# Two-layer hybrid encoder in float32 on one core: conditioning columns load into idle tiles during the feed-forward, and its Strassen sums are gated in the last chunk

## The chip, the cores and the metric

The kernel runs on one core of one Trainium2 chip. The metric is the device time of one execution in microseconds (us); lower is better. The kernel before takes 1888.2 us, the median of three runs between 1886.48 and 1891.04 us.

## What is computed

The reference is a trunk of two layers on one sequence of 512 tokens with 1024 channels, in float32. Cut to what matters here, a layer is:

```python
mod = (silu(c) @ ada_w[l] + ada_b[l])            # six vectors of 1024 from the conditioning vector c
shift_m, scale_m, gate_m, shift_f, scale_f, gate_f = split(mod, 6)
h = rms_norm(x, norm_mix_g[l]) * (1 + scale_m) + shift_m
y = ...                                          # two attention branches, gates, output projection
x = x + gate_m * y
h = rms_norm(x, norm_mlp_g[l]) * (1 + scale_f) + shift_f
x = x + gate_f * (square(relu(h @ w_mlp_up[l])) @ w_mlp_down[l])
```

The last line is the feed-forward: 1024 channels up to 4096 and down to 1024 again. Its result is multiplied by the vector `gate_f` and added to the residual `x`. The six vectors `mod` of a layer are made in 48 pieces of 128 values; the kernel calls each piece a column.

## The kernel before

**Numbers.** Every float32 matrix is split into a high part and a low remainder of a type that TensorE multiplies at full rate, and a product is three matmuls: high by high, high by low, low by high (`mm3`, L265). Each weight tile therefore takes a DMA into a row tile `raw`, an ACT copy to `wh` and a DVE subtraction to `wl` (`split_w`, L249).

**Columns.** `ada` (L141) makes one column. It loads 128 rows of `ada_w` by 1024 (512 KB) into a tile `raw` and DVE multiplies and sums it with the conditioning row in one instruction (the profile's CUSTOM_DVE_ANT_0). Unless told otherwise the tile comes from the pool `rawp`, four buffers that the weight loads use as well.

**Feed-forward.** The loop of L1106 goes over eight chunks `fc` of 512 hidden channels. A chunk first makes its hidden rows (`ups`: four weight tiles `w_up`, 24 matmuls each, then relu, square and split on ACT and DVE), then multiplies them by its part of `w_down`. In chunks below `SEVEN` (six chunks of layer 0, seven of layer 1) this second product is done by Strassen's scheme as seven block products instead of eight. For it DVE forms sums of four `w_down` tiles (`columnside`, two of them in `rawp`), and of the hidden rows (`rowside`). `down7` (L1049) runs the seven products, and `take` moves their results from PSUM into eight sums `y` of 128x512 in SBUF, DVE adding each to what is there. One of the seven products (a12 by b21) is needed only in the first block of the result; it is never moved, and stays in two PSUM banks `zb` of the pool `accp` through all Strassen chunks. `down7` takes the columns of this chunk as a list and calls one at four places (`spare`).

The other chunks are plain. Two row tiles of `w_down` per half of the channels (`cc`) are split, then for each of four blocks `t` of 128 tokens twelve matmuls fill a PSUM bank from `acc()` (two banks of `accp`, three of `ssp`); DVE multiplies the bank by the gate row `gf`, and POOL, in the last chunk DVE, adds it to the residual `x1`. Layer 0 has two plain chunks (6 and 7), layer 1 one (7).

**Where the two meet (L1118).** At the first plain chunk the kernel adds `zb` to the first two sums, multiplies all eight sums by `gf` on DVE and adds them to `x1` on POOL. After the tiles of a plain chunk come its columns (L1172): ten of them in chunk 6 of layer 0.

**Order.** Instructions are handed to a planner, which orders each engine's queue by its own estimate of time, earlier program text first where several could start, and gives out buffers as they become free. Each engine and the DMA queue of SP then run strictly in that order. Only between `order(True)` and `order(False)` is the order that of the text: from the second half of the output projection to the first three `up` blocks, and from the second half (`cc` = 1) of the last chunk of layer 0 through the attention of layer 1, where the RMSNorm of the next layer is woven between the tiles (`norms`, L1160). A column's DVE instruction may not run ahead of the last such stretch (`floor`, L155).

**The pair.** The pool `pp` (L54) has two buffers of 128x1024. Attention uses it for its probabilities; in the feed-forward it holds only the gate row, `gm` during the output projection and `gf` (`grow`, L325) from the first plain chunk on.

Of the kernel before, what the change touches and what calls it, by code (L numbers as in the profile page):

```python
# [10 lines left out]
F32 = mybir.dt.float32  # L11
# [8 lines left out]
D = 1024  # L20
# [4 lines left out]
FCH = 4  # L25
# [16 lines left out]
def trunk(ctx, tc, x, c, pos, cols, rows, ada_w, w_qkv, w_gate, w_ba, w_bb, w_out, w_up, w_down, out):  # L42
# [8 lines left out]
    rawp = pool("raw", 4)  # L51
    wp = pool("w", 5)
    halfp = pool("half", 10)
    pp = pool("p", 2)  # L54
    sp = pool("scr", 2)
    accp = pool("acc", 2, PS)
    ssp = pool("ss", 3, PS)
    tpp = pool("tp", 2, PS)
# [3 lines left out]
    def nosync(after, before):  # L62
        tc.add_manual_dep(after.ins, before.ins.name,
                          mybir.DependencyInfo(mybir.DependencyClass.NoSync,
                                               mybir.DependencyReason.DATA), reason="order")
# [23 lines left out]
    T_, V_, S_, G_ = Ordered(nc.tensor), Ordered(nc.vector), Ordered(nc.scalar), Ordered(nc.gpsimd)  # L89
# [3 lines left out]
    big = lambda shape, dt, name: bigp.tile(shape, dt, name=name, tag="big")  # L93
    turns = [0]

    def acc(wide=True):
        turns[0] += 1
        if wide and turns[0] % 5 >= 2:
            return ssp.tile([128, 512], F32, name="acc", tag="s")
        return accp.tile([128, 512], F32, name="acc", tag="acc")  # L100
# [37 lines left out]
        E_.dma_start(xt, src[t])  # L138
        return xt

    def ada(l, j, far=False, pool_=False):  # L141
        raw = big([128, D], F32, "raw") if far else rawp.tile([128, D], F32, name="raw", tag="raw")
        E_.dma_start(raw, ada_w[l, j])
        m, bias = modT[l][:, j:j + 1], adab[l][:, j:j + 1]

        def add():
            S_.activation(raw, raw, AF.Copy, accum_out=m)
            V_.tensor_add(m, m, bias)

        if pool_:  # L150
            G_.tensor_mul(raw, raw, cbc)
            return add
        else:
            ins = V_.tensor_tensor_reduce(raw, raw, cbc, 1.0, bias, OP.mult, OP.add, m)
            if floor[0] is not None:  # L155
                nosync(ins, floor[0])
# [108 lines left out]
    def mm3(o, sh, sl, mh, ml, start, stop, **more):  # L265
        matmul(o, sh, mh, start=start, stop=False, **more)
        matmul(o, sh, ml, start=False, stop=False, **more)
        matmul(o, sl, mh, start=False, stop=stop, **more)
# [333 lines left out]
    SEVEN = (6, 7)  # L602
# [7 lines left out]
    def prepare(l):  # L610
        hT = []
        return hT, [qkv(l, p, int(p < 6), hT) for p in range(NB_Q)]
# [32 lines left out]
    def first_products(nT, turn, hT, pieces, gslots):  # L645
# [4 lines left out]
        def scales(kt):  # L650
            ada(0, 8 + kt, True)
# [65 lines left out]
    for l in range(DEPTH):  # L717
# [161 lines left out]
        x1 = {}  # L879
        zT = []  # L880
        wb = None
        for j in range(KT):
# [10 lines left out]
            wh, wl = split_w(w_ba[l, j], scale=sg[:, l:l + 1])  # L893
# [5 lines left out]
            zb = sp.tile([128, 512], F32, name="zb", tag="f512", bufs=6)  # L899
# [14 lines left out]
        for cc in range(2):  # L914
# [6 lines left out]
            for t in range(NT):  # L921
                if cc == 0:
                    x1[t] = load_x(t, xsrc)
                ps = acc()
                tk = slice(128 * t, 128 * t + 128)
                for kt in range(KT):
                    wh, wl = w[kt // 2]
                    cw = slice(512 * (kt % 2), 512 * (kt % 2) + 512)
                    mm3(ps, zT[kt][:, 0, tk], zT[kt][:, 1, tk], wh[:, cw], wl[:, cw], kt == 0, kt == KT - 1)
                d = sp.tile([128, 512], F32, name="d", tag="f512", bufs=6)  # L930
# [38 lines left out]
        upturn = [0]  # L969

        def ubank():
            upturn[0] += 1
            pool_, tag = ((ssp, "s"), (pvp, "pv"))[upturn[0] % 2]
            return pool_.tile([128, 512], F32, name="acc", tag=tag)

        def product(banks, u, w, start):

            wh, wl = w
            for i, ps in enumerate(banks):
                for k in range(2):  # L980
                    tk = slice(256 * k + 128 * i, 256 * k + 128 * i + 128)
                    cw = slice(512 * k, 512 * k + 512)
                    mm3(ps, u[:, 0, tk], u[:, 1, tk], wh[:, cw], wl[:, cw], start and k == 0, k == 1,
                        skip_group_check=not start)

        ys, qs, uT, zb = {}, {}, [], []
# [51 lines left out]
        def columnside(fc):  # L1038

            r11, r12, t1, t2 = (big([128, 1024], F32, "raw") for _ in range(4))  # L1040
            r21, r22 = (rawp.tile([128, 1024], F32, name="raw", tag="raw") for _ in range(2))
            for r, (j, k) in ((r11, (0, 0)), (r12, (0, 1)), (r22, (1, 1)), (r21, (1, 0))):
                E_.dma_start(r, w_down[l, fc, k, j])
            V_.tensor_sub(t1, r12, r11)
            V_.tensor_sub(t2, r22, t1)
            V_.tensor_sub(r12, r22, r12)
            return r11, r21, t2, t1, r12, r22
# [48 lines left out]
            take((1, 0), xb)  # L1096


        todo = [lambda i=i: ada(l, i) for i in range(40, 48)]
        counts = [2, 1, 1, 1, 1, 1, 1]  # L1100
        if l + 1 < DEPTH:
            todo += [lambda i=i: ada(l + 1, i) for i in range(24)]
            counts = [3, 3, 4, 4, 4, 4, 10]
        fill = {l: {fc: [todo.pop(0) for _ in range(n)] for fc, n in enumerate(counts)}}

        for fc in range(FC):  # L1106
            last = fc == FC - 1
            if seven(fc):
                w7 = columnside(fc)
            ups(fc, (2, 3) if fc and seven(fc - 1) else range(FCH))  # L1110
            if fc == SEVEN[l]:
                gf = grow(l, 1)
            if seven(fc):
                u7 = rowside(fc)
                ups(fc + 1, (0, 1))
                down7(fc, u7, w7, fill[l].pop(fc, []))
                continue
            if fc == SEVEN[l]:  # L1118
                for b, y in zip(zb, ys[0, 0]):
                    V_.tensor_add(y, y, b)  # L1120
                for (i, cc), y2 in sorted(ys.items()):
                    for k, y in enumerate(y2):
                        xs = slice(512 * cc, 512 * cc + 512)
                        V_.tensor_mul(y, y, gf[:, xs])
                        G_.tensor_add(x1[2 * i + k][:, xs], x1[2 * i + k][:, xs], y)
            if last and l + 1 < DEPTH:
                nxt = prepare(l + 1)
                for i in range(2):
                    nxt[1][0]["load"](i, True)
            for cc in range(2):  # L1130
                w = [split_w(w_down[l, fc, cc, i]) for i in range(2)]
                if last and l + 1 < DEPTH and cc == 0:
                    nxt[1][0]["load"](2)
                ahead = last and cc == 1 and l + 1 < DEPTH
                if ahead:
                    pairs = halves(nxt[0])
                    aT = affine(l + 1, 0)
                    norms = []
                    order(True)
                    nxt[1][0]["load"](3)  # L1140
                for t in range(NT):
                    tk = slice(128 * t, 128 * t + 128)
                    d = sp.tile([128, 512], F32, name="d", tag="f512", bufs=6)
                    final = last and l == DEPTH - 1 and cc == 1 and t == NT - 1
                    for lo, hi in ((0, 256), (256, 512)) if final else ((0, 512),):
                        ps = acc()[:, lo:hi]
                        for f in range(FCH):
                            wh, wl = w[f // 2]
                            cw = slice(512 * (f % 2) + lo, 512 * (f % 2) + hi)
                            mm3(ps, uT[f][:, 0, tk], uT[f][:, 1, tk], wh[:, cw], wl[:, cw], f == 0, f == FCH - 1)  # L1150
                        xs = slice(512 * cc + lo, 512 * cc + hi)
                        V_.tensor_mul(d[:, lo:hi], ps, gf[:, xs])
                        (V_ if last else G_).tensor_add(x1[t][:, xs], x1[t][:, xs], d[:, lo:hi])
                        if last and l == DEPTH - 1:
                            E_.dma_start(out[t, :, xs], x1[t][:, xs])
                    if last and l + 1 < DEPTH and cc == 0:
                        ms[t] = msp.tile([128, 2], F32, name="ms2", tag="ms")
                        square(x1[t], ms[t], 0)
                    if ahead:
                        norms.append(norm(l + 1, 0, t, x1[t], ms[t], aT, pairs))  # L1160
                        if t > 1:
                            norms[t - 2][2]([0])
                        norms[t][0]()
                        E_.dma_start(x2d[t], x1[t])
                        if t > 0:
                            norms[t - 1][1]()
                        if t > 1:
                            norms[t - 2][2]([1])
                if ahead:
                    norms[3][1]()  # L1170
                    early = {1 + i: norms[2 + i][2] for i in range(2)}
            for f in fill[l].pop(fc, []):  # L1172
                f()


_ORDER = ["x", "c", "pos", "cols", "rows", "ada_w", "w_qkv", "w_gate", "w_ba", "w_bb", "w_out", "w_up",
# [64 lines left out]
```

## Time and profile before

| What | Value |
|---|---|
| median of three runs | 1888.2 us |
| the profiled execution, its own time | 1888.52 us |
| its span, first to last instruction | 1886.7 us |
| mean granted TensorE clock | 0.992 |
| ACT, busy | 1021.4 us, 54% of the span |
| DMA, read from memory | 205.09 MB |
| feed-forward of layer 0 | about 613 to 964 us |
| feed-forward of layer 1 | about 1553 to 1883 us |

A row of the groups view names an engine, an operation, the tile written and the tiles read, the shape and the count; behind it stand the busy time, the mean time of one in ns, the idle time of the engine just before such instructions, and what ended it. PE is TensorE, PEld its weight load, DVE VectorE, ACT ScalarE, POOL GpSimd, SP the engine whose queue issues the loads; SPq is that queue. L81 stands on every row, because a helper that records each operation sits there; tile names tell the rows apart. In the view of windows each row is a stretch of time: its length, then for PE, PEld, DVE, ACT and POOL the busy time and the number of instructions, then the granted clock, the busy share of the DMA engines and GB/s. `y` in the attention is another tile than the sums `y` of the feed-forward; the shape 128x512 marks the latter.

### The profile page before, as it was taken

What the parts mean: (1) busy time and instruction counts of PE and PEld (TensorE: products, weight loads), DVE (VectorE), ACT (ScalarE), POOL (GpSimd) and SP (SyncE); (2) the same over time, 40 slices, a digit from 0 to 9 for tenths busy, and PEclk for the clock granted to TensorE, in tenths of its full rate; (3) what the DMA queues carried; (4) which work ended last, traced back from release to release, by engine and by line L of the source; (5) the groups of instructions that cost most, each with busy time, mean ns of one, the idle gap of its engine ahead of it and who ended that gap; (6) DMA issues with size and microseconds to landing.
All of it is one profiled execution on the core that took longest, in us unless ns stands there. A gap on an engine that the chain in (4) does not pass through costs nothing.

```text
span 1886.7 us, 27295 instructions
## 1 busy us (share of the span) xinstructions
PE 1846.5 (98%) x9988; PEld 1632.2 (87%) x9988; DVE 1323.5 (70%) x2357; ACT 1021.4 (54%) x2309; POOL 375.0 (20%) x447
## 2 busy tenths in 40 slices
PE   7999999999999999999899999999999999999998
PEld 5999999998888887878689999999888888888887
DVE  8664567777565778889675465787646567788887
ACT  5565667776434544444355655777662345545541
POOL 4332224422020000001424232343210200000002
PEclk8999999999999999999899999999999999999999
DMA  8421211224563444445322121122136534333331
GB/s 301 136 68 51 60 44 59 61 66 149 201 216 126 135 141 151 151 148 172 118 99 89 35 76 52 42 68 71 45 112 203 190 110 134 123 101 121 102 101 67
DMA packets 63639, 212.09 MB, mean 112 GB/s; under 512 B 7185, under 2 KB 7569, under 8 KB 63506
## 3 DMA queue, kind: packets, MB, share of 16 engines
q1 hardware_dynamic: 63218, 210.27, 34.2%
q8 instruction: 79, 1.29, 0.3%
q14 instruction: 54, 0.44, 0.1%
q10 hardware_dynamic: 288, 0.09, 0.0%
HBM read 205.09 MB, written 5.24 MB: 111 GB/s over the span
## 4 chain that ended last, share of the span: by engine, by line
PE 46%; DVE 10%; DMA 4%; ACT 3%; issue 2%; POOL 1%; DVEq 0%; ACTq 0%; POOLq 0%
PE acc L81 39%; DVE wl L81 3%; PE tp L81 2%; DVE y L81 2%; DVE raw L81 2%; PE s L81 2%; DMA raw<-in_ada_w 2%; PE pv L81 2%; DMA raw<-in_w_up 1%; PE pvb L81 1%; DMA raw<-in_w_down 1%; ACT wh L81 1%; DVE uT L81 1%; DVE s L81 1%; POOL rs L81 1%
## 5 line engine op out<-in xcount | busy, mean ns | idle before, releaser
L81 PE MATMUL acc<-wh,hT 128*128 128x384 f32 x1792 | 517.8, 346 | 6.0 <-ACT hT L81 5.1
L81 ACT ACTIVATE wh<-raw 128x1024 fp32r<-128x1024 f32 (+1 forms) x331 | 324.0, 987 | 321.5 <-PE acc L81 179.1
L81 DVE TENSOR_TENSOR wl<-raw,wh 128x1024 fp32r<-128x1024 f32 (+1 forms) x331 | 378.2, 1153 | 157.9 <-ACT wh L81 157.0
L81 PE MATMUL acc<-hT,wh 128*128 128x512 f32 (+1 forms) x1632 | 482.8, 379 | 5.3 <-ACT wh L81 5.2
L81 PEld LDWEIGHTS acc<-hT,wh 128*128 128x128 f32 x1632 | 298.9, 189 | 61.3 <-ACT wh L81 6.8
L81 PEld LDWEIGHTS acc<-wh,hT 128*128 128x128 f32 x1792 | 330.6, 189 | 12.0 <-ACT hT L81 6.2
L81 PE MATMUL acc<-wh,uT 128*128 128x512 f32 (+1 forms) x928 | 296.4, 393 | 11.1 <-DVE uT L81 7.3
L81 PE MATMUL acc<-hT,wl 128*128 128x512 f32 (+1 forms) x816 | 306.1, 378 | 0.8 <-DVE wl L81 0.7
L81 PE MATMUL acc<-wl,hT 128*128 128x384 f32 x896 | 303.1, 338 | 0.8 <-DVE wl L81 0.8
L81 PEld LDWEIGHTS acc<-wh,uT 128*128 128x128 f32 x928 | 176.0, 190 | 49.8 <-DVE uT L81 8.1
L81 POOL TENSOR_TENSOR rs<-ms,half_neg 128x4 f32<-128x4 f32 (+1 forms) x128 | 123.2, 963 | 476.0 <-DVE ms L81 474.8
L81 PE MATMUL acc<-wl,uT 128*128 128x512 f32 (+1 forms) x464 | 181.1, 390 | 0.0
L81 PEld LDWEIGHTS acc<-hT,wl 128*128 128x128 f32 x816 | 153.6, 188 | 29.9 <-DVE wl L81 1.8
L81 PEld LDWEIGHTS acc<-wl,hT 128*128 128x128 f32 x896 | 169.8, 190 | 4.8 <-DVE wl L81 1.9
L81 DVE CUSTOM_DVE_ANT_0 raw<-raw,cbc,colt 128x1024 f32<-128x1024 f32 x94 | 124.5, 1333 | 52.5 <-DMA raw<-in_ada_w 52.3
L81 POOL TENSOR_TENSOR xt<-xt,y 128x512 f32<-128x512 f32 x16 | 27.4, 1742 | 586.5 <-DVE y L81 586.5
L81 ACT ACTIVATE p<-s,nm 128x512 f32<-128x512 f32 x128 | 86.8, 684 | 64.4 <-DVE nm L81 64.4
L81 PEld LDWEIGHTS acc<-wl,uT 128*128 128x128 f32 x464 | 88.2, 190 | 18.0
L81 DVE TENSOR_TENSOR y<-y,acc 128x512 f32<-128x512 f32 x144 | 94.8, 680 | 11.1 <-PE acc L81 10.6
L81 DVE TENSOR_REDUCE nm<-s 128x1 f32<-128x512 f32 x128 | 82.2, 684 | 28.0 <-PE s L81 27.3
L81 ACT ACTIVATE wT<-tp 128x512 f32<-128x512 f32 (+1 forms) x128 | 65.9, 541 | 45.7 <-PE tp L81 45.7
L81 ACT ACTIVATE T<-y 128x128 fp32r<-128x128 f32 x224 | 68.6, 357 | 39.3 <-POOL y L81 39.3
(158 smaller groups left out, 2820.8 us busy)
## 6 DMA issues: line engine op xcount, KB each, us to landing
raw<-in_ada_w SPq DMA_DIRECT2D x96, 512.0 KB, 4.2
raw<-in_w_qkv SPq DMA_DIRECT2D x112, 384.0 KB, 3.2
raw<-in_w_up SPq DMA_DIRECT2D x64, 512.0 KB, 3.6
raw<-in_w_down SPq DMA_DIRECT2D x64, 512.0 KB, 3.5
raw<-in_w_gate SPq DMA_DIRECT2D x32, 512.0 KB, 3.6
raw<-in_w_ba SPq DMA_DIRECT2D x16, 512.0 KB, 4.4
raw<-in_w_out SPq DMA_DIRECT2D x16, 512.0 KB, 4.1
xt<-in_x SPq DMA_DIRECT2D x8, 512.0 KB, 5.7
```

The source lines that it names most:

```text
L81: ins = f(*a, **k)
```

## The change

Four things are changed. First, the 32 columns made in the feed-forward of layer 0 (eight of its own gate, 24 of layer 1) and the eight of layer 1 load into `pp` in place of `rawp`, four in each of the six Strassen chunks of layer 0 and eight in chunk 6, one after each tile, where it was three, three, four, four, four, four and ten after the tiles. Second, the plain chunk 6 of layer 0 is not gated: its tiles are added to the sums `y` by DVE, and its first two tiles go on accumulating in the held banks `zb`. Third, in the last chunk of each layer every tile is preceded by its own sum's part: DVE multiplies `y` by `gf` and adds it to `x1`; the first two tiles accumulate in `zb` and are gated with it. POOL does none of these adds any more. Fourth, since `zb` keeps the two banks of `accp`, the tiles take banks from `dbank` (`ssp` and `tpp`) until the second half of the last chunk.

```diff
-    def ada(l, j, far=False, pool_=False):
-        raw = big([128, D], F32, "raw") if far else rawp.tile([128, D], F32, name="raw", tag="raw")
+    def ada(l, j, far=False, pool_=False, aside=False):
+        if aside:
+            raw = pp.tile([128, D], F32, name="raw", tag="p")
+        else:
+            raw = big([128, D], F32, "raw") if far else rawp.tile([128, D], F32, name="raw", tag="raw")
...
+        def dbank():
+            upturn[0] += 1
+            pool_, tag = ((ssp, "s"), (tpp, "tp"), (tpp, "tp"))[upturn[0] % 3]
+            return pool_.tile([128, 512], F32, name="acc", tag=tag)
...
-        todo = [lambda i=i: ada(l, i) for i in range(40, 48)]
+        todo = [lambda i=i: ada(l, i, aside=True) for i in range(40, 48)]
         counts = [2, 1, 1, 1, 1, 1, 1]
         if l + 1 < DEPTH:
-            todo += [lambda i=i: ada(l + 1, i) for i in range(24)]
-            counts = [3, 3, 4, 4, 4, 4, 10]
+            todo += [lambda i=i: ada(l + 1, i, aside=True) for i in range(24)]
+            counts = [4, 4, 4, 4, 4, 4, 8]
...
-            if fc == SEVEN[l]:
-                for b, y in zip(zb, ys[0, 0]):
-                    V_.tensor_add(y, y, b)
-                for (i, cc), y2 in sorted(ys.items()):
-                    for k, y in enumerate(y2):
-                        xs = slice(512 * cc, 512 * cc + 512)
-                        V_.tensor_mul(y, y, gf[:, xs])
-                        G_.tensor_add(x1[2 * i + k][:, xs], x1[2 * i + k][:, xs], y)
+            extra = fill[l].pop(fc, [])
...
                 for t in range(NT):
                     tk = slice(128 * t, 128 * t + 128)
-                    d = sp.tile([128, 512], F32, name="d", tag="f512", bufs=6)
                     final = last and l == DEPTH - 1 and cc == 1 and t == NT - 1
+                    y = ys[t // 2, cc][t % 2]
+                    if last:
+                        xs = slice(512 * cc, 512 * cc + 512)
+                        d = sp.tile([128, 512], F32, name="d", tag="f512", bufs=6)
+                        V_.tensor_mul(y, y, gf[:, xs])
+                        V_.tensor_add(x1[t][:, xs], x1[t][:, xs], y)
+                    held = cc == 0 and t < 2
                     for lo, hi in ((0, 256), (256, 512)) if final else ((0, 512),):
-                        ps = acc()[:, lo:hi]
+                        ps = zb[t] if held else (acc() if last and cc else dbank())[:, lo:hi]
...
+                        if not last:
+                            if not held:
+                                V_.tensor_add(y, y, ps)
+                            if extra:
+                                extra.pop(0)()
+                            continue
                         xs = slice(512 * cc + lo, 512 * cc + hi)
                         V_.tensor_mul(d[:, lo:hi], ps, gf[:, xs])
-                        (V_ if last else G_).tensor_add(x1[t][:, xs], x1[t][:, xs], d[:, lo:hi])
+                        V_.tensor_add(x1[t][:, xs], x1[t][:, xs], d[:, lo:hi])
...
-            for f in fill[l].pop(fc, []):
-                f()
```

More of the change, by code (lines that the diff above doesn't have):

```diff
@@ L1149, in trunk @@
                             cw = slice(512 * (f % 2) + lo, 512 * (f % 2) + hi)
-                            mm3(ps, uT[f][:, 0, tk], uT[f][:, 1, tk], wh[:, cw], wl[:, cw], f == 0, f == FCH - 1)
+                            mm3(ps, uT[f][:, 0, tk], uT[f][:, 1, tk], wh[:, cw], wl[:, cw], f == 0 and not held,
+                                f == FCH - 1, skip_group_check=held)
+                        if not last:
[4 more added lines that the diff above has]
+                            continue
                         xs = slice(512 * cc + lo, 512 * cc + hi)
                         V_.tensor_mul(d[:, lo:hi], ps, gf[:, xs])
-                        (V_ if last else G_).tensor_add(x1[t][:, xs], x1[t][:, xs], d[:, lo:hi])
+                        V_.tensor_add(x1[t][:, xs], x1[t][:, xs], d[:, lo:hi])
                         if last and l == DEPTH - 1:
```

## The prediction

> **What bounds the kernel now.** I read the page's engine table first, then PE's waits, then the windows chunk by chunk, then the load queue.
>
> ```profile
> PE 1846.5 (98%) x9988; PEld 1632.2 (87%) x9988; DVE 1323.5 (70%) x2357; ACT 1021.4 (54%) x2309; POOL 375.0 (20%) x447
> ```
>
> TensorE sets the time. The change adds and removes no matmul, so it can gain only where PE stands still or runs slowly in the two feed-forwards. The windows, by chunk: six stretches of the Strassen chunks of layer 0, its passage to the plain chunks, an undisturbed stretch of layer 1, and the end.
>
> ```profile
> 613.00:655.00 42.00, 41.22 (x233) 35.87 (x231) 32.79 (x44) 24.35 (x41) 0.00 (x0) 1.00 0.43 133
> 655.00:696.00 41.00, 40.48 (x177) 33.16 (x178) 32.91 (x41) 20.96 (x30) 0.00 (x0) 1.00 0.41 132
> 696.00:739.00 43.00, 41.07 (x181) 33.72 (x181) 36.28 (x47) 19.89 (x26) 0.00 (x0) 1.00 0.47 147
> 739.00:786.00 47.00, 47.00 (x201) 38.44 (x201) 39.99 (x51) 20.86 (x28) 0.00 (x0) 0.96 0.49 148
> 786.00:824.00 38.00, 36.60 (x161) 29.68 (x160) 32.42 (x41) 18.60 (x25) 0.00 (x0) 1.00 0.45 145
> 824.00:869.00 45.00, 45.00 (x200) 37.26 (x199) 39.53 (x54) 23.18 (x31) 0.00 (x0) 1.00 0.42 138
> 869.00:920.00 51.00, 42.31 (x174) 33.95 (x173) 44.10 (x51) 12.89 (x17) 24.68 (x15) 0.87 0.57 188
> 1655.00:1696.00 41.00, 41.00 (x182) 33.98 (x181) 33.04 (x42) 19.99 (x27) 0.00 (x0) 1.00 0.36 116
> 1858.00:1887.00 29.00, 22.03 (x108) 18.18 (x106) 23.54 (x27) 1.55 (x4) 13.45 (x8) 0.99 0.20 73
> ```
>
> In 1655 to 1696 PE does 182 matmuls in 41.00 us, 0.2253 us each; that is the pace without a stop. By it the matmuls of the other stretches would take 177 × 0.2253 = 39.9 of 41 us, 40.8 of 43, 45.3 of 47, 36.3 of 38, 45.1 of 45: a loss of 1.1, 2.2, 1.7, 1.7 and 0, together 6.7 us. In 613 to 655, where small transposes lie between, I take the idle time, 0.8 us. In 869 to 920 the 174 would take 39.2 of 51: 11.8 us lost, to waits and to a clock granted at 0.87. PE's waits say for what, in layer 0 and then in layer 1:
>
> ```profile
> PE acc L81 <- ACT wh L81: 5.2, 2, 4.4
> PE acc L81 <- DVE uT L81: 4.3, 1, 4.3
> PE acc L81 <- DVE y L81: 3.8, 3, 1.9
> ...
> PE acc L81 <- DVE uT L81: 3.0, 1, 3.0
> ```
>
> So 0.8 + 6.7 + 11.8 + 3.0 = 22.3 us is all that there is to win.
>
> **Why the Strassen chunks of layer 0 lose 7.5 us, and layer 1 none.** The load queue, one chunk of layer 0, its passage, one chunk of layer 1, and DVE's groups in the Strassen chunks of either layer:
>
> ```profile
> 736.43 8.50 SPq L81 DMA_DIRECT2D raw<-in_w_up  x4
> 748.28 7.84 SPq L81 DMA_DIRECT2D raw<-in_ada_w  x4
> 759.27 8.56 SPq L81 DMA_DIRECT2D raw<-in_w_down  x4
> ...
> 871.22 16.38 SPq L81 DMA_DIRECT2D raw<-in_ada_w  x10
> 894.10 12.29 SPq L81 DMA_DIRECT2D raw<-in_w_up  x4
> ...
> 1643.03 0.33 SPq L81 DMA_DIRECT2D raw<-in_ada_w  x1
> 1645.66 15.80 SPq L81 DMA_DIRECT2D raw<-in_w_down  x4
> ```
> ```profile
> L81 DVE TENSOR_TENSOR raw<-raw 128x1024 f32<-128x1024 f32 x24 | 29.2, 1219 | 7.1 <-DMA raw<-in_w_down 7.0
> L81 DVE CUSTOM_DVE_ANT_0 raw<-raw,cbc,colt 128x1024 f32<-128x1024 f32 x22 | 28.2, 1282 | 14.3 <-DMA raw<-in_ada_w 14.3
> ...
> L81 DVE CUSTOM_DVE_ANT_0 raw<-raw,cbc,colt 128x1024 f32<-128x1024 f32 x6 | 7.7, 1285 | 4.5 <-DMA raw<-in_ada_w 4.4
> ```
>
> The four row tiles are given out in the order of the text. In layer 0 four columns stand between the `w_up` tiles and the next `w_down` tiles; DVE, which works in order, waits 14.3 us for them and 7.0 us for the `w_down` behind them, and what it has queued behind those waits is the adds to `y` that free PE's banks. In layer 1 one column stands there, and PE stops nowhere. With the columns in the pair, a chunk asks for six row tiles, not ten. I take the 7.5 us as gone. What would be late next is DVE itself: with four columns of 1.28 us spread over a chunk it has 33.0 + 3 × 1.28 = 36.9 us of work in 41.
>
> **The passage in layer 0 (11.8 us) and in layer 1 (3.0).** DVE's groups in 885 to 911 and 1858 to 1887, and POOL's work:
>
> ```profile
> L81 DVE TENSOR_TENSOR y<-y,grow 128x512 f32<-128x512 f32 x8 | 10.4, 1359 | 0.0
> ...
> L81 DVE TENSOR_TENSOR uT<-q,uT 128x512 fp32r<-128x512 f32 x1 | 1.7, 1744 | 0.0
> ...
> L81 DVE TENSOR_TENSOR y<-y,grow 128x512 f32<-128x512 f32 x8 | 11.5, 1501 | 2.7 <-ACT grow L81 2.7
> ...
> 1858.88 13.45 POOL L81 TENSOR_TENSOR xt<-xt,y 128x512 f32<-128x512 f32 x8 [308.28 <-DVE y L81]
> ```
>
> PE waits for one split `uT`, which stands in DVE's queue behind the eight multiplications of `y`; these take 1359 and 1501 ns beside POOL's adds. In layer 0 ten columns stand there too, and hold the row tiles, so that `w_up` of chunk 7 is asked for only at 894.10: the second wait of 4.4 us, for `wh`. All three causes leave this place: the multiplications go to the last chunk, POOL's adds to DVE, the columns to the pair. I take 11.8 + 3.0 as gone. In the plain chunk of layer 0 the add `y` + bank stands for the multiplication of a bank and two adds of `zb` go, so DVE gets no more there. Tiles find five banks as before (three `ssp`, two `tpp` for two `accp`), and a tile of twelve matmuls (2.7 us) leaves its bank in one DVE operation: no cost.
>
> **What is added.** DVE's groups where layer 0 passes into layer 1 (949 to 977), and PE's wait there:
>
> ```profile
> L81 DVE TENSOR_TENSOR xt<-xt,d 128x512 f32<-128x512 f32 x8 | 5.5, 692 | 0.3
> ...
> L81 DVE CAST hT<-h 128x256 fp32r<-128x256 f32 x12 | 3.5, 298 | 1.8 <-ACT h L81 1.8
> L81 DVE TENSOR_SCALAR n<-xt,rs 128x1024 f32<-128x1024 f32 x4 | 3.0, 749 | 0.5 <-POOL rs L81 0.5
> ...
> 964.26 0.95 PE L81 MATMUL tp<-identr,n 128*128 128x128 f32 x7 [0.22 <-DVE n L81]
> ```
>
> The last chunk gets 16 DVE operations (y times `gf`, then into `x1`) of 0.69 us, 11.0 us. Those of the first half can run early, while PE makes the hidden rows. In layer 0 the eight of the second half stand in the ordered stretch, one pair ahead of each tile, and behind them in DVE's queue the gating, the norm `n` and the splits `hT` for which PE's transposes wait: 5.5 us into gaps of 2.6 us (0.3, 1.8 and 0.5 in these rows). PE already waits 0.22 us for `n` there. The cost lies between 0 and 5.5; no gain is possible, as nothing leaves this stretch. I take 3, 5.5 less the gaps. In layer 1 no order is written and DVE has only `uT` to do from 1858 on: 0.
>
> Then the pace of the columns. In the row tiles their place in the text held them back; in the pair only the pair does. The ten columns at 871, ahead of all tiles of their chunk, show that the planner takes a column as soon as there is a buffer. The 24 columns ahead of `gf` may then come in chunks 0 and 1 instead of six chunks:
>
> ```profile
> raw<-in_ada_w SPq DMA_DIRECT2D x22, 512.0 KB, 3.6
> ...
> DVE raw L81 <- DMA raw<-in_ada_w: 14.3, 12, 3.6
> ```
>
> A turn of a buffer is 3.6 us landing and 1.28 on DVE, so two buffers bring one in 2.4 us, 24 in 59. DVE is busy 32.8 + 32.9 = 65.7 of the 83 us from 613 to 696, of which six columns are 7.7; with 24 (30.8) it would be 88.8, with 14.3/22 = 0.65 us of waiting each 104: over by 21. If the planner spreads them it is 0. I take 4, what the two dearest chunks with four columns lost (2.2 + 1.7).
>
> Last, the eight columns of chunk 6: `gf` holds one buffer of the pair, so they pass one after another through the other, about 5 us each, 40 us for the eight, within the 51 us of the window and the hidden rows of chunk 7; by 0.65 us of waiting each they cost DVE 5 us where the multiplications free 10.4. I take 0; the upper end is a rival.
>
> **Two rules of the Trainium skill.** Of the loss, 1.7 us in 739 to 786 is the granted clock of 0.96 alone, right after the wait of 1.9; I count it as gone with the wait. After the wait of 3.0 in layer 1 the window shows 0.99. The Trainium skill (TensorE: Matmul & The Clock Gate, section "Why this matters for your kernels") puts the drop at pauses of more than about 3 us; by it the 1.7 us would not go with the wait and the sum would be 1875, and here the two rows speak against it. The second rule is on the adds. Beside POOL's adds DVE lost 8 × (1.36 - 0.69) + 8 × (1.50 - 0.69) = 11.8 us on its multiplications, and all 16 adds cost it 16 × 0.69 = 11.0 without POOL, so for DVE the move is even. The Trainium skill (Perfetto Trace Analysis, section "Optimizing Scalar/DVE Operations") says that work of a saturated VectorE may better go to GpSimd, the reverse of this change; by it the 11 us would come back as stops, and the sum would be 1884. The same section warns that the two share a read port, and with that the trace agrees (1359 and 1501 ns against 692).
>
> **The sum.** The profiled execution takes 1888.5, 0.3 over the median. 1888.5 - 22.3 + 3 + 4 - 0.3 = 1872.9: 1873.
>
> **The rivals.**
> Queue: loads still share SP's one queue, and a column that waits for a buffer of the pair holds up the row tiles behind it, as now; or DVE's load of 85% (39.99 of 47, against 33.04 of 41 in layer 1) is the cause and not the waits. Then the change doesn't do in the Strassen chunks what it says, 7.5 stay and only the passages gain: 1873 + 7.5 = 1880. For it: the queue is in order. Against: a column has two buffers and a whole chunk.
> Burst: the 21 us in place of 4: 1890, no change. For it: nothing paces the columns. Against: the planner sees DVE's load and fills only gaps that it sees.
> Slower, through the single buffer: if the planner sets each of the eight columns right behind its tile, DVE stands for each load as long as the longest seen, 3.6 us, with the adds that free the banks behind it: 8 × 3.6 = 29, 1902. It decides from 15/8 = 1.9 us a column on PE's path. Against: the mean wait was 0.65.
>
> **How the numbers follow.** Forecast 0.62, queue 0.20, burst 0.10, single buffer 0.08. A measurement can tell 0.2%, 3.8 us, from no change. Faster is forecast and queue, 0.82; same is burst, 0.10; slower 0.08. The range runs from 1864 (all 22.3 gone with nothing paid is 1866, and pauses of DVE that I didn't count) to 1883, the queue's 1880 with the boundary at its dearer end (5.5 for 3); left out are burst and single buffer.
>
> **What would show it.** Right: no PE wait for `y` in chunks 1 to 5 of layer 0, `w_down` asked for sooner after `w_up`, no `y<-y,grow` above 0.7 us, no PE wait over 1 us between the last Strassen product and the first tiles, granted clock 1.00 in all these windows, POOL empty until the norms. Wrong: PE waits for DVE in chunks 0 and 1 with columns packed there (burst), DVE waits of several us for `in_ada_w` in chunk 6 (single buffer), or waits over 3 us for `n` or `hT` at the start of layer 1.

## The result and the profile after

The kernel after takes 1879.1 us, the median of four runs (1877.97 to 1879.41), beside 1889.05 us for the kernel before on the same chip: a ratio of 0.9947, with a 95% interval from 0.993 to 0.9964. It is 9.9 us faster; 15 were forecast. (The ratios of the experiments below are to runs of the kernel before beside each of them.) The profiled execution has a span 9.1 us shorter. Here is the head of its page:

```profile
span 1877.6 us, 27242 instructions
...
PE 1842.2 (98%) x9988; PEld 1629.5 (87%) x9988; DVE 1313.3 (70%) x2367; ACT 1021.4 (54%) x2309; POOL 335.9 (18%) x423
```

PE does the same matmuls and is busy 4.3 us less, at a mean granted clock of 0.997 for 0.992; the rest of the gain is idle time gone. The windows of the kernel after, cut as before:

```profile
613.00:655.00 42.00, 42.00 (x237) 36.87 (x236) 38.72 (x56) 24.82 (x42) 0.00 (x0) 1.00 0.68 224
655.00:696.00 41.00, 38.41 (x166) 30.32 (x164) 38.08 (x53) 20.38 (x28) 0.00 (x0) 1.00 0.71 241
696.00:739.00 43.00, 38.75 (x158) 31.56 (x159) 35.63 (x45) 18.71 (x25) 0.00 (x0) 0.92 0.34 98
739.00:786.00 47.00, 47.00 (x209) 38.91 (x208) 38.25 (x46) 20.84 (x27) 0.00 (x0) 1.00 0.31 100
786.00:824.00 38.00, 38.00 (x169) 31.49 (x168) 28.83 (x35) 19.79 (x26) 0.00 (x0) 1.00 0.31 98
824.00:869.00 45.00, 45.00 (x200) 37.26 (x199) 34.04 (x44) 23.02 (x30) 0.00 (x0) 1.00 0.29 94
869.00:920.00 51.00, 51.00 (x231) 42.30 (x230) 34.94 (x46) 16.76 (x22) 0.00 (x0) 1.00 0.54 178
```

Two things stand out. The last four rows are what was hoped for: PE is full at clock 1.00, and where the passage did 174 matmuls in 51 us there are now 231. The first three are not. In the first two the DMA engines move 224 and 241 GB/s where they moved 133 and 132, and in the second DVE is busy 38.1 of 41 us for 32.9. In the first PE still keeps up (237 matmuls for 233), but in the second and third it does 166 and 158 where it did 177 and 181, and in the third the clock is down to 0.92. All 24 columns of the six Strassen chunks are summed between 620.62 and 701.65 us, and none from 703 to 890. PE's waits from 613 to 985 us say for whom it stood:

```profile
PE acc L81 <- DVE y L81: 5.2, 3, 4.2
PE tp L81 <- DVE n L81: 2.6, 3, 1.4
PE acc L81 <- DVE wl L81: 2.2, 2, 1.4
PE acc L81 <- ACT wh L81: 0.3, 1, 0.3
```

**Where the time went.** To place gains and losses, one needs an event that every kernel has in the same place of the program. ACT's `r<-acc` serves: it takes a block of hidden rows out of its bank, four times a chunk, 32 times a layer. Here are the last ones of chunk 6 and of chunk 7 in layer 0, on ACT's timeline, in the kernel before:

```profile
883.83 0.60 ACT L81 ACTIVATE r<-acc 128x512 f32<-128x512 f32 x1 [2.34 <-PE acc L81]
...
942.10 0.58 ACT L81 ACTIVATE r<-acc 128x512 f32<-128x512 f32 x1
```

and in the kernel after:

```profile
887.75 0.58 ACT L81 ACTIVATE r<-acc 128x512 f32<-128x512 f32 x1
...
932.42 0.58 ACT L81 ACTIVATE r<-acc 128x512 f32<-128x512 f32 x1
```

The kernel after is 3.9 us late at the first and 9.7 early at the second: the passage gave 13.6. The same subtraction at six places, for the kernel after and for the experiments below, in us against the kernel before (negative is earlier):

| kernel | end of chunk 2 (715.4) | end of chunk 6 (883.8) | end of chunk 7 (942.1) | first block of layer 1 (1567.3) | last block of layer 1 (1856.9) | span |
|---|---|---|---|---|---|---|
| after | +9.2 | +3.9 | -9.7 | -8.0 | -7.8 | -9.1 |
| e1_paced | -1.6 | -4.9 | -18.5 | -16.5 | -14.2 | -15.6 |
| e2_rowtiles | -1.5 | -3.6 | -16.5 | -14.8 | -14.6 | -15.9 |
| e3_pair_only | +6.1 | +0.8 | -5.2 | -1.0 | -1.0 | +0.6 |
| e4_half_sum | +7.7 | +2.4 | -11.2 | -9.5 | -9.3 | -10.6 |
| e5_half_load | +1.0 | -4.2 | -17.9 | -16.2 | -15.9 | -17.2 |
| e6_early_gate | -1.2 | -1.5 | -14.4 | -15.2 | -15.0 | -16.3 |
| e7_tail | -0.2 | +0.7 | -12.1 | -13.0 | -12.8 | -14.4 |
| e8_dve_adds | -1.1 | -0.4 | -4.6 | -5.2 | -5.2 | -8.4 |
| e9_paced_early | -1.3 | -5.8 | -19.4 | -20.4 | -18.7 | -20.0 |
| e10_pool_queue | +5.0 | -0.3 | -13.9 | -12.2 | -12.0 | -13.1 |

Row one is the whole story: 9.2 us lost in chunks 0 to 2, 5.3 regained from there to chunk 6, where no column is left to do, 13.6 won in the passage, 1.7 paid where the layers meet, 1.3 won at the end.

### The profile page after: what moved, and what is told of

It is laid out like the page before. It is cut to its first block, busy times and chain, and to the rows that moved or that the text cites. A ratio compares the mean times of both kernels' runs of the same rounds, so it can differ in the third digit from the quotient of the medians.

```text
span 1877.6 us, 27242 instructions
## 1 busy us (share of the span) xinstructions
PE 1842.2 (98%) x9988; PEld 1629.5 (87%) x9988; DVE 1313.3 (70%) x2367; ACT 1021.4 (54%) x2309; POOL 335.9 (18%) x423
## 4 chain that ended last, share of the span: by engine, by line
PE 85%; DVE 7%; ACT 4%; POOL 2%; issue 2%; DMA 1%; SPq 0%; DVEq 0%; ACTq 0%; POOLq 0%
PE acc L81 71%; PE tp L81 5%; PE s L81 4%; PE pv L81 3%; PE pvb L81 2%; DVE wl L81 2%; POOL rs L81 1%; DVE raw L81 1%; DVE e L81 1%; ACT e L81 1%; ACT T L81 1%; DVE y L81 1%; POOL y L81 1%; DVE ms L81 1%; ACT wh L81 1%
## 5 line engine op out<-in xcount | busy, mean ns | idle before, releaser
L81 PEld LDWEIGHTS acc<-wh,hT 128*128 128x128 f32 x1792 | 329.6, 188 | 13.1 <-ACT hT L81 5.9
L81 DVE TENSOR_TENSOR y<-y,acc 128x512 f32<-128x512 f32 x146 | 96.0, 681 | 18.5 <-PE acc L81 17.9
L81 DVE TENSOR_TENSOR T<-y,T 128x256 fp32r<-128x256 f32 x112 | 51.4, 459 | 53.8 <-ACT T L81 52.2
```

The lines of the kernel that those rows point to most:

```text
L81: ins = f(*a, **k)
```

## The experiments

The theory: late gating wins the passage, and the pair lets the planner pack the columns, which gives back most of what else there was. The rivals: the columns in the row tiles made the passage slow; the packing costs through DVE's time, through the loads, or through SP's queue; POOL's adds slowed DVE by their place in the queue and not by running beside it.

**e1_paced: the kernel after, each column held to its place in the text.**

```diff
+            prev = V_.last
             ins = V_.tensor_tensor_reduce(raw, raw, cbc, 1.0, bias, OP.mult, OP.add, m)
+            if aside:
+                nosync(ins, prev)
```

> The changed kernel with one thing more: each column's DVE instruction is held behind the last DVE instruction written ahead of it, so that the four columns of a chunk stay in their chunk. Theory (burst): the changed kernel made 24 columns between 620 and 702 us and lost there some 10 us of PE time (240 matmuls in 655 to 720 us, 54 us at full pace) that the paced order does not lose: 1868 to 1871 us, no PE wait for y over 0.5 us before 870 us, DVE near 36 us in each 41. Rival (load): four columns a chunk are too much for DVE wherever they stand: the waits of the kernel before return, 1876 to 1880 us.

It takes 1872.8 us, ratio 0.9917 (95% interval 0.9903 to 0.9931), a little more than the 1868 to 1871 expected. Three of its windows:

```profile
655.00:696.00 41.00, 40.97 (x181) 33.66 (x180) 32.90 (x42) 19.28 (x28) 0.00 (x0) 1.00 0.45 139
696.00:739.00 43.00, 43.00 (x191) 35.44 (x190) 38.45 (x50) 20.79 (x28) 0.00 (x0) 1.00 0.48 152
739.00:786.00 47.00, 45.97 (x202) 37.41 (x201) 39.94 (x52) 21.30 (x28) 0.00 (x0) 1.00 0.49 157
```

With four columns to a chunk (139 to 157 GB/s) PE is full again but for 1.0 us in the third of these windows, and the clock stays at 1.00. At the end of chunk 2 it is 10.8 us ahead of the kernel after, at the end of chunk 6 still 8.8. The packing is the cause of the loss. Part of the 10.8 us is the clock, which was granted at half for 6.8 us behind PE's longest wait (the rows are in the last section): 0.92 over 43 us is 3.4 us, a little of it inside the wait itself. In the Strassen chunks of layer 1, where packing had cost nothing, the pace takes 2.3 us back (-16.5 to -14.2).

**e2_rowtiles: the kernel after, its columns back in the row tiles** (`aside=True` taken out of the two lists).

> The changed kernel with the columns back in the four row tiles (late gating, held banks and the new counts stay). Theory: the row tiles pace the columns, so no burst, but the Strassen chunks lose their 7 us again as before; the passage keeps its gain, since the multiplications beside POOL are gone: about 1876 us, with PE waits for y of 1 to 2 us at the same places as in the kernel before. Rival (columns made the passage slow): the eight columns in the row tiles hold w_up of chunk 7 as before, and 4 to 8 us of the passage come back: 1880 to 1885 us.

1873.3 us, 0.9921 (0.9908 to 0.9935), some 3 us better than expected: the pair as built makes the kernel slower, and late gating alone is worth some 15 us. The passage keeps its gain (-3.6 to -16.5: 12.9 us), so with late gating eight columns in the row tiles do it no harm. This does not clear the ten columns of the kernel before; the next run bears on them. PE still waits 3.0 us for `y` in the Strassen chunks, but none of these waits takes the clock down, and they end 3.6 us earlier than before.

**e3_pair_only: the kernel before, its columns in the pair**, with the old counts and the old gating.

> The kernel before with the columns in the pair and nothing else. Theory: burst of some 10 us in chunks 0 and 1, chunks 2 to 5 without waits (6 us won), the passage keeps its wait for uT behind the multiplications beside POOL but loses the wait for wh (4 to 6 us won), the 3.0 us in layer 1 stay: 1885 to 1890 us, about no change. Rival (the passage was slow through the columns alone): 12 us won there: 1880 us.

1888.7 us, 0.9999 (0.9989 to 1.0008). The packing is there without the new gating (+6.1 at the end of chunk 2), and 5.3 come back by chunk 6. The passage is 6.0 us shorter (+0.8 to -5.2), with the old gating and POOL's adds still in it: PE's wait of 4.4 us for `wh` is gone, and the one for `uT` stays, 4.1 us. SP's queue shows why; the kernel before asked for these tiles at 894.10:

```profile
871.28 10.07 SPq L81 DMA_DIRECT2D raw<-in_w_up  x4
```

So the ten columns in the row tiles did cost the kernel before something here. Where the layers meet 4.2 us are lost again: PE waits 2.7 us for `n` and 1.6 for `r`, while the last of the ten columns, which pass one by one through the free buffer of the pair, is summed only at 946.86. That these columns are the reason was not tested by itself. In sum the pair alone is worth nothing.

**e4_half_sum and e5_half_load: DVE's time or the bytes?** The first sums only half of each column of the pair and loads all of it:

```diff
-            ins = V_.tensor_tensor_reduce(raw, raw, cbc, 1.0, bias, OP.mult, OP.add, m)
+            h = 512 if aside else D
+            ins = V_.tensor_tensor_reduce(raw[:, :h], raw[:, :h], cbc[:, :h], 1.0, bias, OP.mult, OP.add, m)
```

The second loads half and keeps DVE as busy, by two sums of 512:

```diff
-        E_.dma_start(raw, ada_w[l, j])
+        if aside:
+            E_.dma_start(raw[:, :512], ada_w[l, j][:, :512])
+        else:
+            E_.dma_start(raw, ada_w[l, j])
...
+                for h in range(2):
+                    ins = V_.tensor_tensor_reduce(raw[:, 512:], raw[:, :512], cbc[:, 512 * h:512 * h + 512], 1.0, bias,
+                                                  OP.mult, OP.add, m)
```

> The changed kernel where a column loaded in the feed-forward is summed over half its row only (512 of 1024 values, which leaves out half of that sum); the loads are the same. DVE's work on a column falls from 1.28 to about 0.68 us, 24 x 0.6 = 14 us less in the burst. Theory (DVE is full in the burst): the waits of chunks 0 and 1 nearly go: 1868 to 1872 us. Rival (the loads of the burst hold the queue of SP and the weights come late): the waits stay: 1876 to 1880 us.

> The changed kernel where a column of the feed-forward loads only half its row (256 KB) and DVE sums that half twice, in two instructions of 512 (this leaves out the other half of the values). DVE's work on a column stays at 2 x 0.68 us; the burst's loads are halved. The kernel with the half sum and the whole load kept 1877 of 1879 us, and there the columns' loads stood on the chain. If the loads of the burst are the price: 1870 to 1873 us. If DVE's queue is full either way: 1877 to 1881 us.

Half the sums: 1877.3 us, 0.9941 (0.9927 to 0.9954). Half the bytes: 1871.35 us, 0.9914 (0.9898 to 0.993). The theory that DVE's time is the price had expected the reverse, and as the whole account it falls. Here is e5_half_load from 655 to 696 us: DVE is busier than in the kernel after (39.93 for 38.08), and PE does 177 matmuls for 166:

```profile
655.00:696.00 41.00, 40.35 (x177) 32.77 (x175) 39.93 (x72) 20.30 (x28) 0.00 (x0) 1.00 0.49 163
```

The view of DMA issues, from 613 to 720 us, gives KB and the median time to landing: first the kernel after, then e4_half_sum, then e5_half_load.

```profile
raw<-in_ada_w SPq DMA_DIRECT2D x22, 512.0 KB, 4.1
...
raw<-in_w_down SPq DMA_DIRECT2D x10, 512.0 KB, 4.5
```
```profile
raw<-in_ada_w SPq DMA_DIRECT2D x22, 512.0 KB, 4.5
...
raw<-in_w_down SPq DMA_DIRECT2D x10, 512.0 KB, 5.3
```
```profile
raw<-in_ada_w SPq DMA_DIRECT2D x22, 256.0 KB, 2.6
...
raw<-in_w_down SPq DMA_DIRECT2D x10, 512.0 KB, 4.0
```

In the kernel before the ten `w_down` loads of this stretch landed in 3.5 us at 143 GB/s.

Neither run isolates one thing. In e4_half_sum PE's longest wait, 4.1 us, is for `wh`, whose `w_up` tile SP asked for at 695.84, behind a run of seven columns. In e5_half_load a buffer of the pair comes free sooner, and with it the order changes too: 19 of the 24 columns are summed by 702 us and the last at 724.7, and SP asks for the second pair of `w_down` tiles sooner than the kernel after does (there at 689.82):

```profile
680.93 1.45 SPq L81 DMA_DIRECT2D raw<-in_w_down  x2
```

**e10_pool_queue: the same loads from another queue.** The loads could cost by their traffic, or because SP's queue is in order. The kernel after asks for the next `w_up` tiles only at 698.89 us, behind a run of columns, where the kernel before did at 693.43:

```profile
674.08 15.64 SPq L81 DMA_DIRECT2D raw<-in_ada_w  x6
689.82 0.86 SPq L81 DMA_DIRECT2D raw<-in_w_down  x2
692.41 0.33 SPq L81 DMA_DIRECT2D raw<-in_ada_w  x1
698.89 2.60 SPq L81 DMA_DIRECT2D raw<-in_w_up  x2
```

```diff
-        E_.dma_start(raw, ada_w[l, j])
+        (G_ if aside else E_).dma_start(raw, ada_w[l, j])
```

> The kernel after, with one thing changed: the loads of the 40 columns of the pair are issued from POOL's queue, which is empty there, in place of SP's. The same 24 columns of 512 KB can be packed into 620 to 702 us. What is open is how the loads cost the burst its 10.6 us, since half the bytes cost nothing. Theory queue: SP's queue is in order, and a column that waits for its buffer holds the row tiles of w_up and w_down behind it; then these are asked for in time here, and the time falls to 1869 to 1873. Theory traffic: the loads share the DMA engines, the row tiles land later (5 us for 3.6) and DVE waits for both, whoever issues them; then the time stays within 3 us of the kernel after, 1876 to 1881, with PE's waits for wh and y at 655 to 702 as before.

1874.1 us, 0.9916 (0.9902 to 0.993): between the two expectations. SP's queue in the same stretch, and PE's wait in it:

```profile
666.68 18.49 SPq L81 DMA_DIRECT2D raw<-in_w_down  x4
695.54 2.06 SPq L81 DMA_DIRECT2D raw<-in_w_up  x2
```
```profile
696.26 0.47 PE L81 MATMUL acc<-wh,uT 128*128 128x512 f32 x1 [3.02 <-DVE y L81]
```

The `w_up` tiles are asked for 3.4 us sooner, and the wait is 3.02 us for 4.25. This edit, too, changes more than the order: the view of DMA issues puts the columns' packets on a second queue of another kind (`software_dynamic`), and POOL is busy 0.53 us with each load. At the end of chunk 2 the kernel is 4.2 us ahead of the kernel after, and 6.6 behind the paced one. So against e1_paced the packing cost 10.8 us by that place; another queue takes 4.2 of it, half the bytes 8.2, half the sums 1.5. So the price is mostly that of the burst of loads and little that of the sums, and the order of SP's queue is a part of it; how much is the bytes as such stays open. The landings give a hint. Those of `w_down` go with the loss: 4.5, 5.3 and 5.0 us in the kernel after, e4_half_sum and e10_pool_queue, but 3.5, 4.0 and 3.9 us in the kernel before, e5_half_load and e1_paced, which lose little or nothing. Those of `w_up` do not: 4.4 us in e10_pool_queue and 4.6 in e1_paced. And in the kernel after the add to `y` for which PE waits 4.25 us stands in DVE's queue behind two splits and a sum of weight tiles, with DVE busy without a stop from 686 us on. That is what six medians and one timeline show together; no run tests it alone.

**e8_dve_adds: the kernel before with one engine changed.** What did POOL's adds do to DVE in the passage?

```diff
-                        G_.tensor_add(x1[2 * i + k][:, xs], x1[2 * i + k][:, xs], y)
+                        V_.tensor_add(x1[2 * i + k][:, xs], x1[2 * i + k][:, xs], y)
```

> The kernel before with one change: the eight sums are added to x1 at the passage by DVE in place of POOL, columns in the row tiles, gating early. Theory (place in the queue): 16 operations of 0.69 us, 11.0 us, stand ahead of uT where now 8 of 1.36 and 1.50 us, 10.4 and 11.5, do: no change, 1887 to 1890 us, the waits for uT stay within 1 us of 4.3 and 3.0. Rival (the shared port is the cause): the multiplications fall to 0.69 us, uT and the columns too, and 5 to 8 us go: 1881 to 1884 us.

1879.4 us, 0.9957 (0.9942 to 0.9971): one word brings 8.8 us, nearly as much as the whole change. I had expected the split `uT` to stand as late in DVE's queue as before; that falls. DVE's groups from 885 to 915 us:

```profile
L81 DVE TENSOR_TENSOR xt<-xt,y 128x512 f32<-128x512 f32 x8 | 5.1, 678 | 0.0
L81 DVE TENSOR_TENSOR y<-y,grow 128x512 f32<-128x512 f32 x8 | 5.0, 682 | 0.0
...
L81 DVE TENSOR_TENSOR uT<-q,uT 128x512 fp32r<-128x512 f32 x1 | 0.7, 678 | 0.0
```

Multiplications of 1359 ns and a split of 1744 ns are 682 and 678 ns once POOL doesn't add beside them. DVE does eight more instructions and is done sooner. PE's waits from 869 to 925 us shrink to these:

```profile
PE acc L81 <- DVE d L81: 2.9, 1, 2.9
PE acc L81 <- ACT wh L81: 2.5, 1, 2.5
```

The 3.0 us wait of layer 1 is gone as well (-5.2 to -8.4 at the end). Late gating adds to this that half of the sums' work, that of the second half of the channels, leaves the passage; the other half runs between the tiles (in the kernel after from 889.02 us on). The wait of 2.5 us for `wh` that is left in e8_dve_adds goes with the columns: they still hold the row tiles, and `w_up` is asked for at 890.88.

**e6_early_gate, e7_tail: the two places where the change pays.** Both start from e2_rowtiles. e6_early_gate gates the second half of the sums ahead of the ordered stretch of layer 0:

```diff
                 if ahead:
+                    for t in range(NT):
+                        y = ys[t // 2, 1][t % 2]
+                        V_.tensor_mul(y, y, gf[:, 512:])
+                        V_.tensor_add(x1[t][:, 512:], x1[t][:, 512:], y)
...
-                        V_.tensor_mul(y, y, gf[:, xs])
-                        V_.tensor_add(x1[t][:, xs], x1[t][:, xs], y)
+                        if not ahead:
+                            V_.tensor_mul(y, y, gf[:, xs])
+                            V_.tensor_add(x1[t][:, xs], x1[t][:, xs], y)
```

e7_tail has this edit as well and adds an ordered stretch at the very end:

```diff
+                if last and cc == 1 and l == DEPTH - 1:
+                    order(True)
```

> The kernel with the columns in the row tiles and the late gating, with one thing moved: the sums of the second half of the last chunk of layer 0 are gated and added ahead of the ordered stretch. Theory: the four pairs of DVE operations in the ordered stretch cost the 2.3 to 2.8 us by which it lags behind the kernel before at the start of layer 1, and that returns: 1870 to 1871 us, no wait of PE for n above 0.3 us. Rival: the lag comes from the four gating pairs of the first half that stand late in DVE's queue: unchanged, 1873 us.

> The kernel with early gating, and the second half of the last chunk of layer 1 in the order of the text. Theory: the changed kernels end 5.6 us after their last matmul, the kernel before 3.7, since the planner finishes the last tiles together and DVE has six or seven operations left; in order it has two: 1.5 us less than with early gating alone, 1869 us. Rival: PE then waits for banks or for gating between the tiles and the gain is lost: same or up to 2 us more.

e6_early_gate: 1872.6 us, 0.9919 (0.9905 to 0.9933). The waits for `n` go:

```profile
PE acc L81 <- DVE y L81: 4.7, 3, 2.4
PE acc L81 <- DVE wl L81: 0.8, 1, 0.8
PE tp L81 <- DVE n L81: 0.2, 1, 0.2
```

The total expected was 1870 to 1871. From chunk 7 to layer 1 it gains 0.8 us where e2_rowtiles loses 1.7: the boundary's price is 2.5. But the waits for `y` in its Strassen chunks, of which it changes nothing, were 4.7 us for 3.0, and the total is the same as e2_rowtiles's within the intervals. e7_tail: 1873.3 us, 0.9922 (0.9909 to 0.9935). From the last block to the end it gains 1.6 us where e6_early_gate gains 1.3; the 1.5 us expected did not come. In its trace DVE works without a stop through the last tiles, with the gating of the sums between them (three multiplications of `y` and three adds after 1861 us); that this is what keeps the end long was not tested.

**e9_paced_early: both mended.** e1_paced with the edit of e6_early_gate.

> The kernel after, with both mended terms together: each column of the pair may not run on DVE ahead of the DVE instruction that stands before it in the text (so no packing into 620 to 702 us), and the sums y of the second half of layer 0's last chunk are gated ahead of the ordered stretch. If the two costs add (packing 10.6 us less what chunks 2 to 5 regain; boundary 2.1 to 2.4), the time is that of the paced kernel less 2.4: 1872.8 - 2.4 = 1870.4, between 1869 and 1872. If the boundary's gain is again eaten by where the Strassen waits happen to fall, as when it was tried with the row tiles, it stays at 1872 to 1873. The waits for n at 950 to 963 should be under 0.5 us in sum either way.

1869.05 us, 0.9894 (0.988 to 0.9907), the fastest: 20 us below the kernel before. PE's waits from 613 to 985 us are down to

```profile
PE acc L81 <- DVE wl L81: 0.8, 1, 0.8
PE tp L81 <- DVE n L81: 0.2, 1, 0.2
```

and the time lies in the range expected if the two costs add (1869 to 1872). Whether the pair, once paced, is worth anything is not clear: e9_paced_early is 3.7 us of span better than e6_early_gate, which differs by the pair and the pace, but e1_paced and e2_rowtiles, which differ by the same, lie at 1872.8 and 1873.3 us.

## Why the prediction came out as it did

Range and direction held; the forecast was 6 us too good. The time, 1879.1, is nearly what the rival "queue" gave (1880), but not by its account: there the Strassen chunks of layer 0 were to keep their old loss of 7.5 us, and in fact the old loss was traded for a new one. That the time fell inside the range is in part luck, for the range was stretched up to 1883 for that rival and not for the burst. By the table, term by term:

| term | predicted | measured | from |
|---|---|---|---|
| Strassen chunks of layer 0, columns paced | -7.5 | -4.9 | e1_paced, end of chunk 6 |
| pace of the columns | +4 | +8.8 | after less e1_paced, end of chunk 6 |
| passage of layer 0 | -11.8 | -13.6 | after, chunk 6 to 7 |
| where the layers meet | +3 | +1.7 | after, chunk 7 to layer 1 |
| Strassen chunks of layer 1 | 0 | +0.2 | after |
| passage of layer 1 and end | -3.0 | -1.3 | after, last block to end |
| sum | -15.3 | -9.1 | |

**The step that failed** is the pace of the columns. Its mechanism was foreseen as the rival "burst": two buffers, all 24 in chunks 0 and 1, one in 3.4 us on the mean (81 us for 24). That happened. The argument against it, that the planner sees DVE's load and fills only gaps, did not hold: DVE was filled to 38 of 41 us. Of the signs named ahead, "no PE wait for `y`" and "clock 1.00" failed here (4.2 us and 0.92), and the sign of the burst, columns packed in front of PE's waits, came. In place of the 4 us taken for it, or the rival's 21, it cost 10.8 us by chunk 2 and 8.8 net. The cost lies between the bounds, 0 and 21, and the value was chosen too near the lower one. The 21 also had a doubtful basis, DVE's time: half of it gave back only 1.5 us (e4_half_sum).

**The Strassen chunks** of layer 0 gave less than was counted. In the kernel before PE waited 4.6 us from 613 to 869 us (3.8 for `y`, 0.8 for `wh`), and the clock took 1.7: 6.3 us, where the prediction counted 7.5. In e9_paced_early PE has no wait left there, and it ends chunk 6 5.8 us earlier; in e1_paced it waits 1.0 us and ends 4.9 earlier. So the pair, once paced, does here what was forecast, and the term was 1 to 2 us too large. With late gating and the columns in the row tiles PE waits 3.0, 4.7 and 5.8 us for `y`, and the chunks end 3.6 and 1.5 us earlier and 0.7 later than in the kernel before (e2_rowtiles, e6_early_gate, e7_tail), though the text of these chunks is the same in all three. So an edit elsewhere shifts them by up to 4 us, for a reason that stays open, and the row tiles' share is anything from 1 to 6.5 us by these runs.

**The passage** was sized well, and its three causes were real, but their prices do not add. POOL's adds moved alone gave 4.2 us there and 3.2 in layer 1 (e8_dve_adds); the columns moved alone gave 6.0 there (e3_pair_only); late gating, which takes POOL's adds out too, gave 12.9 with the columns still in the row tiles (e2_rowtiles), and all together 13.6. One reason is the clock. Of PE's waits, 8.7 us in the kernel before, either is followed by matmuls at half clock, so what removes a wait also wins some clock:

```profile
900.08:913.72 13.64, 7.85 (x18) 5.70 (x19) 13.64 (x15) 2.11 (x2) 8.25 (x6) 0.50 0.51 167
```

In the kernel after DVE's groups from 885 to 960 us show the multiplications at their short time:

```profile
L81 DVE CUSTOM_DVE_ANT_0 raw<-raw,cbc,colt 128x1024 f32<-128x1024 f32 x8 | 10.3, 1283 | 9.3 <-DMA raw<-in_ada_w 9.3
...
L81 DVE TENSOR_TENSOR y<-y,grow 128x512 f32<-128x512 f32 x8 | 5.4, 685 | 0.0
```

The first row judges the rival "single buffer": DVE did stand 9.3 us for the eight columns of chunk 6, against the 29 feared, and PE waited for nothing there (231 matmuls in 51 us). The rival "queue" is right in part, inside the burst only (e10_pool_queue).

**The boundary** came as worked out, a little cheaper: three waits for `n`, 2.6 us, where 3 of at most 5.5 were taken; e6_early_gate takes all but 0.2 us of them away.

**The end** was costed at nothing, and it cost 1.7. The 3.0 us wait went. But after the last matmul the kernel before ran 3.7 us more and the kernel after 5.6. PE's last row in the latter, and DVE's last rows:

```profile
1871.69 0.28 PE L81 MATMUL acc<-wh,uT 128*128 128x256 f32 x1
```
```profile
1870.58 1.62 DVE L81 TENSOR_TENSOR d<-acc,grow 128x512 f32<-128x512 f32 x3 [1.30 <-PE acc L81]
1872.12 0.68 DVE L81 TENSOR_TENSOR xt<-xt,d 128x512 f32<-128x512 f32 x1
1872.71 0.42 DVE L81 TENSOR_TENSOR d<-acc,grow 128x256 f32<-128x256 f32 x1
1873.05 1.35 DVE L81 TENSOR_TENSOR xt<-xt,d 128x512 f32<-128x512 f32 x3
```

Three banks are gated one behind the other while PE does its last matmuls, and their adds stand behind PE's end. That the missing written order is why is not shown, since e7_tail wrote one and won 0.3 us.

**The two rules.** The adds: the Trainium skill (Perfetto Trace Analysis, section "Optimizing Scalar/DVE Operations") says that moving work of a full VectorE to GpSimd may make sense, and warns that, since the two share a read port, it might not help; e8_dve_adds decides for the warning here, by 8.8 us, and the 1359 and 682 ns agree with it. The clock: the 1.7 us of the window at 0.96 did go with its wait of 1.9, as counted, but the burst's wait of 4.2 us brought 3.4 us of the same kind into the window from 696 to 739 us.

## What to carry to other kernels

Loads moved out of contended buffers into idle ones lose the brake that those buffers were: if a planner places them, give them a pace, or it may fetch all at once, and here the urgent loads were then asked for later and landed later. An add that looks free on an idle GpSimd is not free if VectorE works beside it with both inputs in SBUF; price both engines in that stretch, and try the one-word move first. A change made of several parts should be timed part by part: here one part won 15 us and another gave some 6 of it back.

## What the runs showed of the hardware

Not every VectorE operation suffers beside GpSimd's adds. In the kernel before `y<-y,grow`, with both inputs in SBUF, doubled to 1359 ns; in e8_dve_adds, where POOL still adds `d` to `xt` from 904 us on, `d<-acc,grow`, with one input in PSUM, took 677 ns, while the split `wl`, with both in SBUF, took 1523 ns on the mean of four, for 1221 in the kernel after.

The granted clock after a pause of PE followed no single length. It fell to half and stayed there for 3.4 us behind a pause of 1.93 us (the kernel before), and for 6.8 us behind one of 4.25 us (the kernel after) and behind two of 3.02 and 1.05 us (e10_pool_queue). In the kernel after it fell before the pause was over and came back in one step:

```profile
739.66:743.06 3.40, 3.40 (x10) 2.62 (x9) 2.62 (x4) 1.87 (x2) 0.00 (x0) 0.50 0.32 120
```
```profile
700.59:707.40 6.81, 5.52 (x13) 4.39 (x14) 6.81 (x10) 2.11 (x2) 0.00 (x0) 0.50 0.43 143
707.42:712.00 4.58, 4.58 (x21) 3.77 (x21) 4.32 (x7) 0.33 (x1) 0.00 (x0) 1.00 0.55 131
```
```profile
697.61:704.42 6.81, 5.75 (x15) 4.22 (x14) 6.81 (x10) 2.11 (x2) 1.06 (x2) 0.50 0.71 256
```

Behind the 2.4 us of e6_early_gate it stayed at 1.00:

```profile
739.00:786.00 47.00, 44.56 (x197) 36.35 (x195) 38.94 (x49) 20.80 (x28) 0.00 (x0) 1.00 0.45 140
```

From 702 to 712 us of the kernel after PE did 33 matmuls where at 0.2253 us each 44 fit: the pause of 4.25 us cost some 2.5 us more. The Trainium skill (TensorE: Matmul & The Clock Gate, section "Why this matters for your kernels") puts the drop at pauses of more than about 3 us; the pauses of 4.25 and 3.02 agree, the one of 1.93 does not.
